# Transformer block: six modulation tiles of the mixer's stream taken during the input projection's last six output tiles, and silu(c)'s copy stored there

## The chip, the cores and the metric

The kernel runs on one core of a Trainium2 chip, in one launch. The metric is the device time of that core in microseconds (us). The engines are TensorE (PE in the profile, its weight loads PEld), VectorE (DVE), ScalarE (ACT), GpSimd (POOL) and SyncE (SP, which here issues most of the DMA transfers). Each engine works through its own list of instructions in order and waits on semaphores where it needs another's result.

## What is computed

One layer of a diffusion transformer: 512 latent tokens and 256 context tokens of width 2048, in float32.

```python
mod_l = (silu(c) @ w_ada + b_ada)          # 6 x 2048 numbers: 96 tiles of 128
mod_c = (silu(c_ctx) @ w_ada + b_ada)      # of which 32 tiles are used
sh_a, sc_a, gt_a, sh_f, sc_f, gt_f = split(mod_l, 6)
h_l = rms_norm(x) * (1 + sc_a) + sh_a      # and h_c from ctx with mod_c
qa, kva, kr, cb, cc, ch = split(h @ w_in)  # for both streams
att_l = attention(q_l, [k_l, k_c], [v_l, v_c])     # 8 heads
conv_l = cb_l * dwconv3(cc_l * ch_l)
x = x + gt_a * (rms_norm([att_l, conv_l]) @ w_out)
hf = rms_norm(x) * (1 + sc_f) + sh_f
u = dwconv3(hf @ w_up); a, g = split(u, 2)
x = x + gt_f * ((a * silu(g)) @ w_down)
return rms_norm(x)
```

The 96 tiles of mod_l are the modulation tiles: tile t is 128 columns of w_ada, multiplied by silu(c) and summed over 2048 rows. Tiles 0 to 31 (shift and scale of the mixer) are needed for h_l, 32 to 47 (gt_a) by the output projection's residual, 48 to 79 for hf, 80 to 95 at the very end.

## The kernel before, in words

The activations lie transposed in SBUF: 16 tiles of 128 features by 512 tokens. A product keeps nearly float32 accuracy by splitting each operand into a high part (a cast on ScalarE, line 166 for weights, 337 for activations) and the remainder (a subtraction on VectorE, lines 167 and 338), and takes three matmuls (lines 187 to 189: high x high, high x low, low x high). So each weight block costs one operation on ScalarE and one on VectorE before TensorE can use it.

A modulation tile isn't computed on TensorE. Its 1 MB of w_ada is loaded as two halves of 128x1024, and VectorE multiplies each half with a copy of silu(c) (`sv`, 128x2048, the same row in each partition) and sums along the row, all in one instruction with an accumulator: two dots a tile, 1.22 us each by the profile. For mod_l's tiles 0 to 31 this is line 241 in the input projection, for the context's 32 tiles line 530, for the tiles from 32 on line 263. The state of that late stream is the dictionary `late`: `late_load` starts the next tile's load, `late_dot` does one of its two dots, `late_both` both and the load of the next one. Each fourth tile the sums are added up (lines 268 and 269).

The program's phases, in order of time:

1. Start: x is loaded and squared, silu(c) becomes `sv`; then the first dots.
2. Input projection (loop at line 564). The 16 rows of the contraction are taken in three chunks `ci` of 2, 4 and 10. Per chunk, first six output tiles together (`pf`), then the other 25 of ORDER one by one (`pp`): load `rw{ci}_{m}`, split, matmuls, `evac`. In chunk 2 the context's modulation tiles (`cm`, `ctx_mods`) are dotted, one for each output tile. They run out before the last six output tiles, m = 25 to 30. Around these stand the low-rank norms (`low_rank`, line 394), the short convolution (lines 467 to 474), and the context's normalised tiles cr and hc (lines 515, 516, 343, 344).
3. Attention. It begins with the query parts pq00, pq02 and pq01 of head pair 0 (`q_nope`); pq02 is copied to `xq0` on ScalarE, and TensorE's rotation `qr0` (line 379) reads that copy. Then come the three context tiles (pc0 to pc2, weights wc), and 32 steps of softmax, in which the late stream takes 22 tiles (from t = 32 on) by 1 MB loads `ra`.
4. Output projection: 28 steps of `late_both` and `whole` take the late stream's other 34 tiles, the last of them during the halves of output tiles 14 and 15 (o140, o150, o141, o151); after that the residual (line 980), the second norm, and the preparation of hf (`hf_tile`).
5. Up projection, convolution, down projection. The last eight modulation tiles, 88 to 95, are done beside these with silu(c) loaded again from `sv_d` in DRAM (line 1291), since the SBUF space of `sv` is given up at the end of the output projection. The store to `sv_d` is line 1009.

What sets the order: a scheduler decides, by its own estimate of times, which instruction stands where on each engine's list. Only what is wrapped in `keep` holds its program order among the kept instructions of its engine: the dots of the late and the context's stream, and, until the end of chunk 1, every load of `fetch_to`. The store of line 1009 is not wrapped, and the scheduler has put it to the start of SP's list, as soon as `sv` is there. The pool `p_sb` has four buffers with the tag "ada" for the halves of modulation tiles; a load waits until the dot of the buffer's earlier content is done, and SP's list waits with it.

## Time and profile before

| what | us |
|---|---|
| median of 3 runs | 2135.92 (2135.22 to 2137.73) |
| the profiled execution, its own time | 2139.37 |
| its span, first to last instruction | 2137.6 |
| busy in it: TensorE | 2091.0 |
| VectorE | 1826.5 |
| ScalarE | 1047.5 |
| GpSimd | 117.2 |

The profile shows one execution, so its times are set against its own 2139.37 us and not against the median. A row of the timeline has the start in us, the duration, the engine, the line of the kernel, the operation, output and inputs, how many neighbouring instructions are put together, and in brackets the idle time ahead of it and what ended that. A row's duration can overlap the next row's start (the engines are pipelined), so the pitch from start to start is what a row costs in a dense stretch. A row of the windows has the stretch, its length, the busy time of PE, PEld, DVE, ACT and POOL with the number of instructions, the granted TensorE clock (1.00 is full), the DMA engines' busy share and GB/s.

### The profile page before, as it was taken

Reading aid. Unit: us, or ns where it says so; the run is one execution under the profiler, and the core shown is the slowest. Engines: PE = TensorE matmul, PEld = TensorE weight load, DVE = VectorE, ACT = ScalarE, POOL = GpSimd, SP = SyncE. Lnnn points to the kernel's source line nnn. Section 1 sums busy time; section 2 is a strip of 40 time slices with the busy share of each in tenths; the row PEclk is TensorE's granted clock in tenths of the full one; section 3 lists DMA queues with packets and bytes.
Section 4 is the critical chain, followed back from the end, with each engine's and each line's share of the span. In section 5 each row is a group of like instructions: output and inputs, shape, how many; then the busy total and the mean of one; then the engine's idle time right before and its main releaser. Section 6 shows DMA issues by size and latency. Waiting matters only on the chain.

```text
span 2137.6 us, 35318 instructions
## 1 busy us (share of the span) xinstructions
PE 2091.0 (98%) x13268; PEld 1881.8 (88%) x13268; DVE 1826.5 (85%) x3024; ACT 1047.5 (49%) x1715; POOL 117.2 (5%) x144
## 2 busy tenths in 40 slices
PE   7999999999999999999999999999999999999997
PEld 4688788888988888999999999999999889999997
DVE  7998987778896989898999999999999658888887
ACT  5533333555552337565555555555655433333445
POOL 0000000000000100011000000000000000000000
PEclk9999999999999999999999999999999999999999
DMA  8989886334459986577788888788888989878684
GB/s 331 343 279 329 276 275 195 126 128 152 166 188 353 348 283 220 142 217 207 230 238 232 233 233 244 224 234 234 235 229 229 362 306 307 250 231 239 197 236 134
DMA packets 170177, 513.75 MB, mean 240 GB/s; under 512 B 18963, under 2 KB 23315, under 8 KB 164371
## 3 DMA queue, kind: packets, MB, share of 16 engines
q1 hardware_dynamic: 133364, 418.14, 57.7%
q0 software_dynamic: 17408, 59.25, 14.1%
q10 hardware_dynamic: 19232, 34.09, 4.2%
q8 instruction: 104, 1.70, 0.3%
q14 instruction: 69, 0.56, 0.1%
HBM read 464.22 MB, written 46.14 MB: 239 GB/s over the span
## 4 chain that ended last, share of the span: by engine, by line
PE 90%; DVE 4%; DMA 3%; ACT 2%; issue 1%; SPq 0%; DVEq 0%; ACTq 0%; POOLq 0%
PE pp L187 4%; PE pp L189 4%; PE pp L188 4%; PE d L187 1%; PE o L187 1%; PE d L188 1%; PE o L188 1%; PE d L189 1%; PE o L189 1%; PE uf L187 1%; PE uf L189 1%; PE uf L188 1%; PE of L187 1%; PE of L188 1%; PE of L189 1%; PE pf L188 1%
## 5 line engine op out<-in xcount | busy, mean ns | idle before, releaser
L1151 POOL DMA_DIRECT2D u_s<-in_w_up x80 | 68.6, 857 | 684.0 <-DMA u_s<-in_w_up 378.1
L263 DVE SCALAR_TENSOR_TENSOR ada<-ada,sv 128x1024 f32<-128x1024 f32 x68 | 82.1, 1220 | 11.4 <-DMA ada<-in_w_ada 11.2
L166 ACT CAST w_0h<-rw 128x512 fp32r<-128x512 f32 (+1 forms) x63 | 38.3, 618 | 108.3 <-PE pp L188 67.6
L241 DVE SCALAR_TENSOR_TENSOR ada<-ada,sv 128x1024 f32<-128x1024 f32 x64 | 77.6, 1220 | 2.2 <-DMA ada<-in_w_ada 2.1
L530 DVE SCALAR_TENSOR_TENSOR ada<-ada,svc 128x1024 f32<-128x1024 f32 x64 | 76.0, 1219 | 2.5 <-DMA ada<-in_w_ada 2.4
L167 DVE TENSOR_TENSOR w_0l<-rw,w_0h 128x512 fp32r<-128x512 f32 (+1 forms) x63 | 42.7, 683 | 22.8 <-ACT w_0h L166 22.6
L263 DVE SCALAR_TENSOR_TENSOR ra<-ra,sv 128x1024 f32<-128x1024 f32 x44 | 52.5, 1219 | 1.1 <-DMA ra<-in_w_ada 1.1
L1265 DVE TENSOR_TENSOR u<-u,u_s 128x1024 f32<-128x1024 f32 x40 | 48.8, 1220 | 0.7 <-DMA u_s<-in_w_up 0.5
L1266 DVE TENSOR_TENSOR u<-u,u 128x1024 f32<-128x1024 f32 x40 | 48.7, 1218 | 0.0
L793 POOL TENSOR_TENSOR gr<-gr,half 128x8 f32<-128x8 f32 x4 | 10.1, 2524 | 630.1 <-DVE gr L792 538.2
L764 ACT CAST pth<-t 128x384 fp32r<-128x384 f32 x64 | 28.6, 485 | 26.4 <-PE t L761 26.4
L1075 DVE TENSOR_TENSOR tp<-a,tp 128x256 fp32r<-128x256 f32 x90 | 37.7, 419 | 3.3 <-ACT tp L1074 3.3
L1074 ACT CAST tp<-a 128x256 fp32r<-128x256 f32 x90 | 35.7, 403 | 5.5 <-DMA yl6h<-y_d 4.2
L1038 ACT ACTIVATE g<-g 128x512 f32<-128x512 f32 x43 | 27.3, 634 | 18.3 <-DVE g L1032 18.0
L541 DVE TENSOR_TENSOR acc<-acc,pp 128x512 f32<-128x512 f32 x50 | 34.1, 683 | 2.1 <-PE pp L189 2.1
L765 DVE TENSOR_TENSOR ptl<-t,pth 128x384 fp32r<-128x384 f32 x64 | 33.2, 550 | 2.6 <-ACT pth L764 2.6
L745 DVE TENSOR_REDUCE mn<-s 128x1 f32<-128x768 f32 x32 | 30.4, 953 | 4.9 <-PE s L734 4.6
L1030 ACT ACTIVATE g<-cg,sm 128x512 f32<-128x512 f32 x40 | 32.6, 815 | 0.0
L1030 ACT ACTIVATE a<-ca,sm 128x512 f32<-128x512 f32 x40 | 32.1, 802 | 0.0
L748 ACT ACTIVATE p<-s,mn 128x768 f32<-128x768 f32 x32 | 29.3, 916 | 1.6 <-DVE mn L745 1.3
L1031 DVE SCALAR_TENSOR_TENSOR g<-cg,sm,g 128x511 f32<-128x511 f32 x40 | 29.8, 746 | 0.0
L1032 DVE SCALAR_TENSOR_TENSOR g<-cg,sm,g 128x511 f32<-128x511 f32 x40 | 29.8, 746 | 0.0
(10238 smaller groups left out, 8925.0 us busy)
## 6 DMA issues: line engine op xcount, KB each, us to landing
ada<-in_w_ada SPq DMA_DIRECT2D x196, 512.0 KB, 5.7
u<-in_w_up SPq DMA_DIRECT2D x120, 512.0 KB, 8.9
w<-t_d SPq DMA_DIRECT2D x161, 256.0 KB, 5.3
u_s<-in_w_up SPq DMA_DIRECT2D x80, 512.0 KB, 4.0
u_s<-in_w_up POOLq DMA_DIRECT2D x80, 512.0 KB, 9.6
t_d<-tp ACTq DMA_DIRECT2D x126, 256.0 KB, 5.9
v<-in_w_dnw SPq DMA_DIRECT2D x72, 384.0 KB, 5.1
ra<-in_w_ada SPq DMA_DIRECT2D x22, 1024.0 KB, 4.8
```

The costliest lines, as they stand in the source:

```text
L166: A.copy(out=hi[:, :n], in_=raw[:, a:a + n])
L167: V.tensor_tensor(out=lo[:, :n], in0=raw[:, a:a + n], in1=hi[:, :n].bitcast(F32), op=ALU.subtract)
L187: PE.matmul(ps, w[0], x[0], start=first, stop=False, skip_group_check=on_top)
L188: PE.matmul(ps, w[0], x[1], start=False, stop=False, skip_group_check=on_top)
L189: PE.matmul(ps, w[1], x[0], start=False, stop=last, skip_group_check=on_top)
L241: V.scalar_tensor_tensor(out=r, in0=r, scalar=1.0, in1=vec[:, i * 1024:(i + 1) * 1024], op0=ALU.mult, op1=ALU.mult, accum_out=col[:, i:i + 1])
L263: keep(V.scalar_tensor_tensor(out=r, in0=r, scalar=1.0, in1=svs[i], op0=ALU.mult, op1=ALU.mult, accum_out=lc[:, t % 4:t % 4 + 1] if i else ...
L530: keep(V.scalar_tensor_tensor(out=raw[q], in0=raw[q], scalar=1.0, in1=svc[:, q * 1024:(q + 1) * 1024], op0=ALU.mult, op1=ALU.mult, accum_o ...
L1030: A.activation(u, src, AF.Identity, bias=s("fb", m), scale=s("fw", 86 + m))
L1151: G_.dma_start(r[-1], src[more], accum_op=ALU.add)
L1265: V.tensor_tensor(out=a11, in0=a11, in1=s1, op=ALU.add)
L1266: V.tensor_tensor(out=a12, in0=a12, in1=a11, op=ALU.add)
```

## The change

```diff
                 if ci == 2:
                     for q in range(2 if i % 4 == 0 else 1):
                         next(cm, None)
+                    if i == 18:
+                        late_load(ada_load)
+                        keep(SP.dma_start(sv_d, sv))
+                    elif i > 18:
+                        late_both(ada_load if i < len(ORDER) - G - 1 else None)
                     if i >= 5 and i % 2 == 1 and (i - 5) // 2 < CTX_EARLY:
                         bg.append(ctx_prep((i - 5) // 2))
                     pump(2)
...
     assert late["t"] == late["end"] and late["raw"] is None
-    SP.dma_start(sv_d, sv)
     ph1.close()
```

The loop variable i counts the 25 single output tiles of chunk 2; i = 18 is m = 6, and 19 to 24 are m = 25 to 30. At i = 18 the load of modulation tile 32 and the store to `sv_d`, now kept in order, are issued. At each of the six that follow, one tile is dotted (t = 32 to 37) and, except at the last, the next one loaded into the "ada" buffers. The attention then takes 38 to 59 (as many as before), and the output projection 60 to 87, 28 tiles where it took 34.

SP's list at the start of the program, before (rf00 are the first weights of the input projection, ada170 is the first half of modulation tile 17):

```order
L145 DMA ada00_235<-in_w_ada 128x1024
L145 DMA ada01_237<-in_w_ada 128x1024
L145 DMA rf00_251<-in_w_in 128x1536
L1009 DMA sv_d_81<-sv_93 128x2048
L145 DMA ada170_283<-in_w_ada 128x1024
L145 DMA ada171_285<-in_w_ada 128x1024
L145 DMA ada10_291<-in_w_ada 128x1024
```

And now, at the same place:

```order
L145 DMA ada00_235<-in_w_ada 128x1024
L145 DMA ada01_237<-in_w_ada 128x1024
L145 DMA rf00_251<-in_w_in 128x1536
L145 DMA ada170_283<-in_w_ada 128x1024
L145 DMA ada171_285<-in_w_ada 128x1024
L145 DMA ada10_291<-in_w_ada 128x1024
```

The store is gone from there. It now stands in SP's list near the end of the input projection, between the load of modulation tile 32 (ada320 and ada321) and the weights of output tile 26:

```order
L145 DMA ada150_2884<-in_w_ada 128x1024
L145 DMA ada151_2886<-in_w_ada 128x1024
L145 DMA ada320_2994<-in_w_ada 128x1024
L145 DMA ada321_2996<-in_w_ada 128x1024
L608 DMA sv_d_81<-sv_93 128x2048
L145 DMA rw2_26_3080<-in_w_in 128x1280
L145 DMA ada330_3057<-in_w_ada 128x1024
L145 DMA ada331_3059<-in_w_ada 128x1024
```

The store has moved by some 170 places in SP's list, and the loads of the late stream stand ahead of and between the weights of the last tiles.

ScalarE's list in the start, before, from the first activated tile to the first narrow weights (w0_13h and w0_15h are casts of rw0_13):

```order
L438 ACTIVATE xr0_113<-xr0_113,mod_90,sc0_244 128x512
L337 CAST h0h_247<-xr0_113 128x512
L438 ACTIVATE xr1_117<-xr1_117,mod_90,sc1_300 128x512
L166 CAST w0_13_0h_339<-rw0_13_337 128x512
L166 CAST w0_15_0h_384<-rw0_13_337 128x512
L166 CAST w0_17_0h_406<-rw0_13_337 128x512
```

And now:

```order
L438 ACTIVATE xr0_113<-xr0_113,mod_90,sc0_244 128x512
L337 CAST h0h_247<-xr0_113 128x512
L166 CAST w0_13_0h_339<-rw0_13_337 128x512
L166 CAST w0_15_0h_384<-rw0_13_337 128x512
L438 ACTIVATE xr1_117<-xr1_117,mod_90,sc1_300 128x512
L337 CAST h1h_303<-xr1_117 128x512
```

Two casts of weights have moved ahead of xr1's activation; on VectorE, in the same stretch, h0l has moved behind the three dots ada171, ada10 and ada11.

VectorE's list at the end of the input projection, before: from the context tile cr10 to qr0y, which reads the rotation qr0:

```order
L515 TENSOR_TENSOR cr10_3397<-cg5_3391,rc_220 128x256
L515 TENSOR_TENSOR cr11_3403<-cg5_3391,rc_220 128x256
L344 TENSOR_TENSOR hc10_3400<-cr10_3397,hc10_3400 128x256
L344 TENSOR_TENSOR hc11_3406<-cr11_3403,hc11_3406 128x256
L338 TENSOR_TENSOR q00l_3437<-pq00_3423,q00h_3436 128x512
L167 TENSOR_TENSOR wc00_0l_3534<-rc0_3530,wc00_0h_3533 128x512
L541 TENSOR_TENSOR acc30_710<-acc30_710,pp2_29_3259 128x512
L167 TENSOR_TENSOR wc04_0l_3551<-rc0_3530,wc04_0h_3550 128x512
L474 TENSOR_TENSOR acc30_710<-acc30_710,acc29_695 128x512
L167 TENSOR_TENSOR wc08_0l_3570<-rc0_3530,wc08_0h_3569 128x512
L381 TENSOR_TENSOR qr0y_3461<-qr0_3459,kc_83 128x512
```

And now, the same part of the list, which is longer (acc30 is the evacuation of output tile 30, ada370 and ada371 are the two halves of modulation tile 37):

```order
L515 TENSOR_TENSOR cr7_3406<-cg3_3394,rc_220 128x256
L167 TENSOR_TENSOR wq01l_3513<-rq01_3456,wq01h_3512 128x512
L541 TENSOR_TENSOR acc30_710<-acc30_710,pp2_29_3290 128x512
L263 SCALAR_TENSOR_TENSOR ada370_3324,mod_90<-ada370_3324,sv_93 128x1024
L263 SCALAR_TENSOR_TENSOR ada371_3326,lc_94<-ada371_3326,sv_93 128x1024
L471 SCALAR_TENSOR_TENSOR acc29_695<-acc28_686,sm_82,acc29_695 128x511
L344 TENSOR_TENSOR hc6_3403<-cr6_3400,hc6_3403 128x256
L344 TENSOR_TENSOR hc7_3409<-cr7_3406,hc7_3409 128x256
L167 TENSOR_TENSOR wc00_0l_3573<-rc0_3569,wc00_0h_3572 128x512
L167 TENSOR_TENSOR wc04_0l_3590<-rc0_3569,wc04_0h_3589 128x512
L472 SCALAR_TENSOR_TENSOR acc29_695<-acc28_686,sm_82,acc29_695 128x511
L167 TENSOR_TENSOR wc08_0l_3609<-rc0_3569,wc08_0h_3608 128x512
```

```order
L515 TENSOR_TENSOR cr8_3418<-cg4_3412,rc_220 128x256
L515 TENSOR_TENSOR cr9_3424<-cg4_3412,rc_220 128x256
L474 TENSOR_TENSOR acc30_710<-acc30_710,acc29_695 128x512
L344 TENSOR_TENSOR hc8_3421<-cr8_3418,hc8_3421 128x256
L344 TENSOR_TENSOR hc9_3427<-cr9_3424,hc9_3427 128x256
L515 TENSOR_TENSOR cr10_3436<-cg5_3430,rc_220 128x256
L515 TENSOR_TENSOR cr11_3442<-cg5_3430,rc_220 128x256
L344 TENSOR_TENSOR hc10_3439<-cr10_3436,hc10_3439 128x256
L344 TENSOR_TENSOR hc11_3445<-cr11_3442,hc11_3445 128x256
L338 TENSOR_TENSOR q00l_3476<-pq00_3462,q00h_3475 128x512
L381 TENSOR_TENSOR qr0y_3500<-qr0_3498,kc_83 128x512
```

Dots stand between the evacuations and what follows them, and the context tiles cr8 to cr11, which stood ahead of acc30, now stand behind it and behind the last two dots.

ScalarE's list there, before, from cr10's activation to the copy xq0:

```order
L516 ACTIVATE cr10_3397<-cr10_3397,modc_91,scc5_3395 128x256
L516 ACTIVATE cr11_3403<-cr11_3403,modc_91,scc5_3395 128x256
L343 CAST hc10_3400<-cr10_3397 128x256
L343 CAST hc11_3406<-cr11_3403 128x256
L337 CAST q00h_3436<-pq00_3423 128x512
L166 CAST wc00_0h_3533<-rc0_3530 128x512
L166 CAST wc04_0h_3550<-rc0_3530 128x512
L166 CAST wc08_0h_3569<-rc0_3530 128x512
L652 COPY xq0_3457<-pq02_3444 128x512
```

And now:

```order
L516 ACTIVATE cr10_3436<-cr10_3436,modc_91,scc5_3434 128x256
L516 ACTIVATE cr11_3442<-cr11_3442,modc_91,scc5_3434 128x256
L343 CAST hc10_3439<-cr10_3436 128x256
L343 CAST hc11_3445<-cr11_3442 128x256
L337 CAST q00h_3475<-pq00_3462 128x512
L657 COPY xq0_3496<-pq02_3483 128x512
```

The three weight casts of the first context tile (wc) stand ahead of cr8 now, and the copy follows q00h directly.

VectorE's list at the end of the output projection, before, from the last weight remainder of o151 to the residual of tile 15:

```order
L167 TENSOR_TENSOR o151w1536l_7579<-o15r1_7261,o151w1536h_7578 128x512
L263 SCALAR_TENSOR_TENSOR ada860_7370,mod_90<-ada860_7370,sv_93 128x1024
L980 SCALAR_TENSOR_TENSOR x14_7265<-ol0_7263,mod_90,x14_7265 128x256
L263 SCALAR_TENSOR_TENSOR ada861_7372,lc_94<-ada861_7372,sv_93 128x1024
L263 SCALAR_TENSOR_TENSOR ada870_7408,mod_90<-ada870_7408,sv_93 128x1024
L355 TENSOR_TENSOR fq0t_6497<-fq0t_6497,fq14_7508 128x256
L291 RECIPROCAL rr_7488<-rr_7488 128x2
L263 SCALAR_TENSOR_TENSOR ada871_7410,lc_94<-ada871_7410,sv_93 128x1024
L268 TENSOR_TENSOR mod_90<-mod_90,lc_94 128x4
L269 TENSOR_TENSOR mod_90<-mod_90,sm_82 128x4
L980 SCALAR_TENSOR_TENSOR x15_7267<-ol1_7264,mod_90,x15_7267 128x256
```

And now, from the same remainder on; the residual of tile 15 comes a few rows later:

```order
L167 TENSOR_TENSOR o151w1536l_7580<-o15r1_7292,o151w1536h_7579 128x512
L291 RECIPROCAL rr_7489<-rr_7489 128x2
L985 SCALAR_TENSOR_TENSOR x14_7296<-ol0_7294,mod_90,x14_7296 128x256
L355 TENSOR_TENSOR fq0t_6538<-fq0t_6538,fq14_7509 128x256
L962 TENSOR_TENSOR x0_6535<-x0_6535,rl_92 128x256
L962 TENSOR_TENSOR x1_6541<-x1_6541,rl_92 128x256
L282 SCALAR_TENSOR_TENSOR fs2_7860<-mod_90,sm_82 128x1
L282 SCALAR_TENSOR_TENSOR fs3_7884<-mod_90,sm_82 128x1
L967 TENSOR_TENSOR hf0l_7549<-x0_6535,hf0h_7548 128x256
L962 TENSOR_TENSOR x2_6548<-x2_6548,rl_92 128x256
L946 TENSOR_TENSOR hf10_7576<-x1_6541,hf10_7576 128x256
L962 TENSOR_TENSOR x3_6555<-x3_6555,rl_92 128x256
```

The dots are gone from there, and the first tiles of hf (x0 to x3, hf0l, hf10) have moved ahead of the residual of tile 15. TensorE's list is unchanged in its matmuls; a few of them are interleaved otherwise at the start, at the end of the input projection and at the end of the output projection.

## The prediction

> **What bounds the kernel now.** I read the busy times on the page first, then the chain of waits, then the timelines of the three places where the order of instructions differs.
>
> ```profile
> PE 2091.0 (98%) x13268; PEld 1881.8 (88%) x13268; DVE 1826.5 (85%) x3024; ACT 1047.5 (49%) x1715; POOL 117.2 (5%) x144
> PE 90%; DVE 4%; DMA 3%; ACT 2%; issue 1%; SPq 0%; DVEq 0%; ACTq 0%; POOLq 0%
> ```
>
> TensorE is busy for 98% of the span and is 90% of the chain that ends last. Its matmuls are the same before and after, so the change can only lengthen or shorten the few stretches in which TensorE waits or runs at a lower clock. VectorE, at 85%, is close behind: where it gets more work it can become what TensorE waits for. The change moves twelve dot products and twelve 512 KB loads from the output projection's end to the input projection's end, and a 1 MB store out of the start. So there are three places to price.
>
> **Place 1, the start: the store leaves a crowded SP queue.** The store's code stands at the end of the output projection, but the trace has it at the start of the program.
>
> ```profile
> 15.56 0.33 SPq L145 DMA_DIRECT2D rf<-in_w_in  x1
> 16.22 0.33 SPq L1009 DMA_DIRECT2D sv_d<-sv  x1
> 24.00:32.00 8.00, 4.11 (x13) 3.15 (x14) 7.05 (x14) 4.49 (x8) 0.00 (x0) 1.00 1.02 414
> 29.61 0.69 DVE L338 TENSOR_TENSOR h0l<-xr,h0h 128x512 fp32r<-128x512 f32 x1 [0.39 <-ACT h0h L337]
> 36.31 1.29 DVE L167 TENSOR_TENSOR w_0l<-rw,w_0h 128x512 fp32r<-128x512 f32 x2 [1.39 <-ACT w_0h L166]
> 42.29 1.22 DVE L241 SCALAR_TENSOR_TENSOR ada<-ada,sv 128x1024 f32<-128x1024 f32 x1
> 43.96 0.38 SPq L145 DMA_DIRECT2D rw<-in_w_in  x1
> DMA to landing us min/median/max: 8.5/8.9/9.2
> 52.88 0.62 ACT L166 CAST w_0h<-rw 128x512 fp32r<-128x512 f32 x1 [5.96 <-DMA rw<-in_w_in]
> 54.03 0.50 PE L187 MATMUL pp<-h0h,w_0h 128*128 128x512 f32 x1 [1.91 <-ACT acc L539]
> 57.30 0.80 PE L187 MATMUL pp<-h0h,w_0h 128*128 128x512 f32 x1 [1.23 <-ACT acc L539]
> 54.00:56.00 2.00, 1.97 (x6) 1.14 (x6) 2.00 (x5) 2.00 (x5) 0.00 (x0) 0.78 1.02 416
> 56.00:58.00 2.00, 0.77 (x3) 0.61 (x3) 2.00 (x4) 2.00 (x5) 0.00 (x0) 0.50 1.05 436
> 60.00:62.00 2.00, 2.00 (x6) 1.58 (x5) 2.00 (x8) 0.00 (x0) 0.00 (x0) 0.51 0.83 330
> ```
>
> In the window from 24 to 32 the DMA engines are full (share 1.02, 414 GB/s), so 1 MB less is about 2.5 us of transfer (1.05 MB by 414 GB/s) that everything behind it doesn't wait for. That alone gains nothing unless TensorE is held by it. It is, later: the second weight load of the narrow tiles, rw0_21, is issued at 43.96, right behind the dot that begins at 42.29 and frees a buffer in the same SP queue. It takes about 8.9 us to land, and ScalarE sits idle for 5.96 us until its cast at 52.88. Behind that cast stands the copy that frees a PSUM bank, and TensorE idles 1.91 and 1.23 us at 54.03 and 57.30 for such copies, after which the clock is 0.50.
>
> In the new order on VectorE h0l, which waited 0.39 us for its cast, stands behind three dots, and ScalarE casts the first narrow weights ahead of xr1's activation, so the 1.39 us idle at 36.31 is filled too. The dots then end 0.39 + 1.39 = 1.8 us earlier: rw0_21 is issued at about 42.2 and lands at about 51.1. ScalarE now has three casts and one activation of 0.5 to 0.7 us each ahead of the first copy (2.3 us), so that copy is at 53.4 as before, and TensorE goes on at 54.0. But the second copy, which came after three more casts and an activation, now has nothing ahead of it: TensorE goes on at about 55.6, right behind its 1.5 us of matmuls, where it was 57.30. That is **1.7 us gained**. The lower clock from 54 to 62 cost up to 3.4 us (2 x (0.22 + 0.50 + 0.50 + 0.49), the stretch from 58 to 60 taken like that before it); with one gap of 1.9 us in place of two it may vanish or stay, and I take 1.4 of it. **Term 1: -3.1.** Its bounds: 0, if the load's landing isn't brought forward; -1.7 - 3.4 = -5.1, if all of the lower clock goes.
>
> **Place 2, the end of the input projection: the dots move in.** Each dot is two rows of VectorE work; the rows before give all the pitches.
>
> ```profile
> 352.26 1.22 DVE L530 SCALAR_TENSOR_TENSOR ada<-ada,svc 128x1024 f32<-128x1024 f32 x1
> 353.41 1.22 DVE L530 SCALAR_TENSOR_TENSOR ada<-ada,svc 128x1024 f32<-128x1024 f32 x1
> 354.55 0.42 DVE L167 TENSOR_TENSOR w_8l<-rw,w_8h 128x256 fp32r<-128x256 f32 x1
> 354.89 0.68 DVE L355 TENSOR_TENSOR klt<-klt,kl 128x512 f32<-128x512 f32 x1
> 355.49 0.69 DVE L167 TENSOR_TENSOR w_0l<-rw,w_0h 128x512 fp32r<-128x512 f32 x1
> 386.40 0.40 PE L189 MATMUL pp<-h15h,w_8l 128*128 128x512 f32 x1
> sum 56.00, PE 55.20 PEld 44.59 DVE 41.67 ACT 26.56 POOL 0.00; mean PE 3.94 PEld 3.19 DVE 2.98 ACT 1.90 POOL 0.00
> 396.00:400.00 4.00, 4.00 (x19) 3.25 (x18) 3.27 (x7) 2.88 (x6) 0.00 (x0) 1.00 0.83 295
> 400.95 0.76 DVE L515 TENSOR_TENSOR cr<-cg,rc 128x256 f32<-128x256 f32 x2 [0.58 <-DMA cg<-in_ctxt]
> 403.02 0.58 ACT L337 CAST q00h<-pq 128x512 fp32r<-128x512 f32 x1
> 407.53 0.58 ACT L652 COPY xq<-pq 128x512 f32<-128x512 f32 x1
> 406.81 0.39 PE L189 MATMUL pq<-qa3h,wq02l 128*128 128x512 f32 x1
> 408.17 1.12 PE L379 MATMUL qr<-xq,kc 128*128 128x512 f32 x2 [0.97 <-ACT xq L652]
> ```
>
> A dot has a pitch of 1.15 us (352.26 to 353.41), a 128x256 operation 0.34 (354.55 to 354.89), a 128x512 one 0.60. The sum row is that of the windows from 352 to 408: VectorE is busy for 41.67 of 56 us, so it has 14.3 us free, and twelve dots take 12 x 1.15 = 13.8. On the mean they just fit; but half of them stand late. From the evacuation of tile 28 (acc28) to cr11, the new order has 45 rows on VectorE: 6 dots, 21 of 128x512, 2 of 128x511, 13 of 128x256, 3 tiny ones. That is 6 x 1.15 + 21 x 0.60 + 2 x 0.66 + 13 x 0.34 + 0.3 = 25.5 us without a single wait. Tile 28's last matmul ends at 386.8, so cr11 ends at 412.3 at the earliest; before, it was done at 401.7 (400.95 + 0.76).
>
> What hangs on cr11: ScalarE takes cr11's activation, two casts, the cast q00h, and only then the copy xq0 (in the order before three weight casts stood between q00h and the copy, now none). Before, q00h ended 1.8 us after cr11. So the copy starts at about 412.3 + 1.8 = 414.1 rather than 407.53, and TensorE's rotation (L379), which started 0.64 after the copy, at 414.7 rather than 408.17: 6.5 later. TensorE is done with its work ahead of the rotation at 407.2 (406.81 + 0.39) in both orders, and behind it stand pq01 and the context tiles. So TensorE idles some 7.5 us where it idled 0.97. The loads are not what is late: the fullest of these windows, 396 to 400, has a DMA share of 0.83. In SP's queue the store now stands ahead of tile 26's weights, and can hold them by 2.5 us at most (the transfer at the start's rate); the twelve loads wait for buffers that the dots free, and the weights of tiles 27 to 30 stand behind them. TensorE has no wait for weights here before, and a late tile would only take a part of the stall forward, since VectorE's 25.5 us stay.
>
> A wait of that length costs clock too.
>
> ```profile
> 620.97 0.36 PE L187 MATMUL po<-pth,v30h 128*128 128x256 f32 x1 [1.48 <-DVE den L791]
> 622.68 0.58 PE L188 MATMUL po<-ptl,v30h 128*128 128x256 f32 x1 [1.35 <-DVE ptl L765]
> 622.00:624.00 2.00, 1.32 (x6) 1.32 (x7) 2.00 (x5) 1.70 (x4) 0.00 (x0) 0.50 0.79 310
> 630.00:632.00 2.00, 2.00 (x6) 1.54 (x5) 2.00 (x4) 1.60 (x4) 0.00 (x0) 0.50 1.01 358
> 814.35 0.61 PE L316 MATMUL rs<-io,fq0t 128*128 128x1 f32 x4 [2.85 <-DVE fq0t L355]
> 815.83 0.39 PE L187 MATMUL uf<-hf0h,ufw0h 128*128 128x256 f32 x1 [0.88 <-ACT ufw0h L1023]
> 816.00:818.00 2.00, 2.00 (x12) 2.00 (x13) 2.00 (x5) 2.00 (x4) 0.00 (x0) 0.58 1.02 408
> 818.00:820.00 2.00, 2.00 (x12) 2.00 (x12) 2.00 (x7) 1.82 (x5) 0.00 (x0) 0.57 1.02 409
> ```
>
> After idles of 1.48 and 1.35 us the clock was 0.50 for five windows, 622 to 632: 10 us at half speed, 5.0 lost. After one of 2.85 and one of 0.88 it was 0.58 and 0.57 for 4 us: 4 x 0.425 = 1.7 lost. The new idle is a single long one, so I take the row nearest in form, 1.7, and keep 5.0 as the far end.
>
> The Trainium skill, page "TensorE: Matmul & The Clock Gate", section "Part 1: The HAM clock gate", says that the clock is halved after an idle window of about 3.4 us and restored after one of steady work, the windows running freely; by that rule the stall would cost 3.4 us at half speed, an estimate of 1.7 lost. The trace agrees at 816 to 820 and differs at 622 to 632, where the half clock followed waits of under 1.5 us and lasted three times as long.
>
> **Term 2: 6.5 + 1.7 = +8.2.** Bounds: 0, if VectorE's rows ahead of cr11 don't bind; 6.5 + 5.0 = +11.5.
>
> **Place 3, the step to the up projection: the dots leave.**
>
> ```profile
> 811.12 0.38 PE L299 MATMUL rs<-io,rr 128*128 128x128 f32 x2
> 811.27 1.23 DVE L263 SCALAR_TENSOR_TENSOR ada<-ada,sv 128x1024 f32<-128x1024 f32 x1 [0.80 <-DMA ada<-in_w_ada]
> 812.82 0.48 DVE L980 SCALAR_TENSOR_TENSOR x<-ol,mod,x 128x256 f32<-128x256 f32 x1
> ```
>
> The last matmul of the output projection is over at about 811.3, but the residual that reads it starts at 812.82, since a dot that waited for its load stands ahead of it on VectorE. TensorE's next matmul (814.35) follows the residual by 1.53. Without the dots the residual starts at about 811.4, and L316 at about 813.0 rather than 814.35; the first matmul of the up projection then waits for its weight cast and not for anything of the dots, and I put it at 814.0 rather than 815.83. **Term 3: -1.8.** Bounds: -0.5, if the weights' landing holds it; -3.5, if the 1.7 of lower clock behind it goes too (1.8 + 1.7).
>
> **Of no cost:** the store and the twelve loads in their new place (the windows' free DMA share hides them, as said), the 22 loads during the attention (as many as before), the later dots.
>
> **Sum:** -3.1 + 8.2 - 1.8 = +3.3. The profiled execution took 2139.37 us, 1.8 more than its span of 2137.6 and 3.45 more than the median of the runs, 2135.92. So it would be 2142.7 on its own scale, and 2135.92 + 3.3 = **2139.2** on that of the runs. About 0.2% (4.3 us, 2131.6 to 2140.2) is what a measurement of this kernel can tell from no change.
>
> **Rivals.**
> - *The stall doesn't arise* (chance 0.21). If VectorE has caught up before cr11, because its rows ahead of acc28 run early and the long operations overlap more than their pitch says, the second term is 0: -3.1 - 1.8 = -4.9, so 2131.0, faster. For it: the 14.3 us free against 13.8 needed. Against it: tile 28's end, from which the 25.5 us are counted, is fixed by TensorE.
> - *The half clock stays long* (0.13; the other side, slower). The mechanism of 622 to 632 at the rotation: +6.5 + 5.0 - 3.1 - 1.8 = +6.6, so 2142.5. It decides from 2.7 us of loss on (6.5 + 2.7 - 3.1 - 1.8 = 4.3), which is 5.4 us at half clock. For it: the longest stretch in the trace followed much shorter idles. Against it: the 4 us at 816.
> - *The store was not in the way* (0.14). The change doesn't gain at the start what moving the store promises: if rw0_21 waits for something else than the dots in the queue, term 1 is 0, and +8.2 - 1.8 = +6.4 gives 2142.3. For it: TensorE's first matmul waits for ScalarE's h0h rather than for a load, and the new order puts three dots ahead of h0l. Against: the 5.96 us wait at 52.88 is on a DMA.
>
> **How the numbers follow.** The forecast has 0.52, of which 0.33 lies within 0.2% and 0.19 above it, since 2139.2 is only 1.0 under the upper edge. The first rival gives 0.17 faster and 0.04 within; the second 0.13 slower; the third 0.06 within and 0.08 slower. Together faster 0.17, same 0.43, slower 0.40. The range runs from the first rival's time, less 0.5 for a start that gains more, 2130.5, to 2145.6, which is the bounds of terms 2 and 3 (+11.5 - 1.8 = +9.7) with no gain at the start; half of the first rival and the extremes of the others lie outside, under 2 in 10. The forecast's own range is 2136 to 2142.
>
> **What would show it.** At the start: rw0_21 issued at 42.2 and not 43.96, and TensorE's wait at 57.3 gone; wrong if both stay. At the input projection's end: dots on VectorE without a gap from tile 28 to cr11, the copy xq0 near 414 and a wait of 7 us at L379 (less whatever the start has gained in time), with a half clock behind it; wrong if that wait is under 3 us. At the step: the residual of x15 within 0.3 us of the last matmul. What would make the sum wrong as a whole: a wait in the attention that moves with the dots' new tile numbers, which I price at nothing.

## The result, and the profile after

| | before | changed |
|---|---|---|
| median, us (6 runs each, same chip) | 2136.38 (2134.61 to 2137.73) | 2146.47 (2141.82 to 2148.41) |
| changed / before | | 1.0045, 95% interval 1.0032 to 1.0058 |
| the profiled execution, us | 2139.37 | 2148.41 |
| its span, us | 2137.6 | 2146.5 |

The change makes the kernel slower by some 10 us; 2139.2 was forecast, with a range to 2145.6. In the profiled executions the spans differ by 8.9 us. To see where, the start of the same TensorE instruction is taken in both timelines. A difference that grows between two rows is time lost there.

| TensorE starts | before, us | changed, us | later by |
|---|---|---|---|
| chunk 1 of the input projection (pf1) | 86.18 | 83.48 | -2.70 |
| first gp5, end of output tile 29 | 393.61 | 394.58 | +0.97 |
| the rotation qr0 (L379) | 408.17 | 419.95 | +11.78 |
| first key product pkl00 | 430.92 | 445.30 | +14.38 |
| output projection (of) | 628.03 | 643.91 | +15.88 |
| up projection (uf) | 815.83 | 829.82 | +13.99 |
| down projection, sliding part (v0a) | 1756.21 | 1768.97 | +12.76 |
| last norm | 2127.03 | 2135.97 | +8.94 |

The busy times of the page look like those of before, and its chain of waits has the same shares; they don't show where 9 us went:

```profile
PE 2089.4 (97%) x13268; PEld 1878.7 (88%) x13268; DVE 1825.8 (85%) x3024; ACT 1048.9 (49%) x1715; POOL 117.1 (5%) x144
```

**The start.** The rows of the SP queue, of ScalarE, of TensorE and of the windows that answer to those of place 1, and the wait at the step into chunk 2:

```profile
42.64 0.38 SPq L145 DMA_DIRECT2D rw<-in_w_in  x1
52.27 1.14 ACT L166 CAST w_0h<-rw 128x512 fp32r<-128x512 f32 x2 [6.94 <-DMA rw<-in_w_in]
54.53 0.57 ACT L539 COPY acc<-pp 128x512 f32<-128x512 f32 x1
55.16 0.50 PE L187 MATMUL pp<-h0h,w_0h 128*128 128x512 f32 x1 [3.31 <-ACT acc L539]
56.00:58.00 2.00, 2.00 (x10) 1.44 (x9) 2.00 (x4) 1.61 (x4) 0.00 (x0) 1.00 0.81 311
223.53 0.51 PE L189 MATMUL pp<-h6h,w_0l 128*128 128x512 f32 x1 [2.01 <-DVE w_0l L167]
224.00:226.00 2.00, 2.00 (x7) 1.55 (x6) 2.00 (x4) 0.00 (x0) 0.00 (x0) 0.59 0.91 349
```

The weights rw0_21 are issued 1.3 us earlier than before, there is one wait (3.31 us) in place of two, and the clock stays at 1.00: TensorE is 2.7 us ahead at 83.48. At 223.53 it waits 2.01 us for a weight remainder of VectorE and then runs at half clock: 1.0 + 1.7 us are gone again. The same wait in the kernel before:

```profile
224.71 0.50 PE L189 MATMUL pp<-h6h,w_0l 128*128 128x512 f32 x1 [1.06 <-DVE w_0l L167]
```

**The end of the input projection.** The SP queue, ScalarE, VectorE, TensorE, windows:

```profile
390.51 1.47 SPq L145 DMA_DIRECT2D ada<-in_w_ada  x2
393.20 3.99 SPq L145 DMA_DIRECT2D rq<-in_w_q  x2
397.88 0.62 ACT L166 CAST wq02h<-rq 128x512 fp32r<-128x512 f32 x1 [2.33 <-DMA rq<-in_w_q]
398.56 0.79 PE L187 MATMUL pq<-qa0h,wq02h 128*128 128x512 f32 x1 [2.68 <-ACT wq02h L166]
406.57 0.69 DVE L167 TENSOR_TENSOR wq01l<-rq,wq01h 128x512 fp32r<-128x512 f32 x1 [2.10 <-ACT wq01h L166]
416.79 0.75 DVE L515 TENSOR_TENSOR cr<-cg,rc 128x256 f32<-128x256 f32 x2
419.32 0.58 ACT L657 COPY xq<-pq 128x512 f32<-128x512 f32 x1
419.95 2.07 PE L379 MATMUL qr<-xq,kc 128*128 128x512 f32 x2 [7.33 <-ACT xq L657]
400.00:402.00 2.00, 2.00 (x6) 1.57 (x5) 2.00 (x4) 0.00 (x0) 0.00 (x0) 0.54 0.00 0
420.00:422.00 2.00, 2.00 (x3) 0.97 (x4) 0.14 (x1) 0.00 (x0) 0.00 (x0) 0.50 0.03 8
```

Two waits stand here: 7.33 us for the copy xq0, as foreseen, and 2.68 us for the query weights wq02h, which was not. The row at 393.20 puts two loads together: the first is that of wq02, the second, at 396.86, that of wq01. The load of wq02 lands at 397.79, 4.6 us after its issue, where it took 2.6 us before. Ahead of it in the queue stands modulation tile 37 (390.51); its second half could be issued only at 391.65, when a dot had freed its buffer, and lands 0.7 us ahead of wq02. Each wait has half clock behind it. Together 2.68 + (7.33 - 0.97) + 1.6 + 2.9 (the time that TensorE worked at half clock between 398 and 402 and between 420 and 426, halved) = 13.5, and the table has 14.38 - 0.97 = 13.4.

The weights wq02 are also needed sooner than before. VectorE's remainder qa0l of the queries' first input tile and the first matmuls of wq00 and wq02, before and then now:

```profile
385.71 0.69 DVE L338 TENSOR_TENSOR qa0l<-acc,qa0h 128x512 fp32r<-128x512 f32 x1
394.42 0.48 PE L187 MATMUL pq<-qa0h,wq00h 128*128 128x512 f32 x1
397.28 0.40 PE L187 MATMUL pq<-qa0h,wq02h 128*128 128x512 f32 x1
```

```profile
399.78 0.68 DVE L338 TENSOR_TENSOR qa0l<-acc,qa0h 128x512 fp32r<-128x512 f32 x1
395.40 0.48 PE L187 MATMUL pq<-qa0h,wq00h 128*128 128x512 f32 x1
```

Before, twelve matmuls of wq00 (2.9 us) stand ahead of the first of wq02. Now there is only one, and qa0l to qa3l, which four of the others read, stand behind dots on VectorE. So the few matmuls that are interleaved otherwise bear on the cost, though no run has the dots with the order of before (and TensorE's list also differs at places in the attention, between 490 and 610 us).

**The end of the attention and the step to the up projection.** TensorE's timeline, VectorE's residual of tile 15, and a window:

```profile
630.41 0.83 PE L766 MATMUL t<-io,p 128*128 128x128 f32 x3 [2.08 <-DVE ptl L770]
639.44 0.36 PE L187 MATMUL po<-pth,v30h 128*128 128x256 f32 x1 [3.55 <-DVE ptl L770]
827.26 0.48 DVE L985 SCALAR_TENSOR_TENSOR x<-ol,mod,x 128x256 f32<-128x256 f32 x1 [0.39 <-PE ol L189]
828.87 0.61 PE L316 MATMUL rs<-io,fq0t 128*128 128x1 f32 x4 [1.65 <-DVE fq0t L355]
829.82 0.39 PE L187 MATMUL uf<-hf0h,ufw0h 128*128 128x256 f32 x1 [0.34 <-ACT ufw0h L1027]
830.00:832.00 2.00, 2.00 (x18) 2.00 (x19) 2.00 (x4) 2.00 (x4) 0.00 (x0) 1.00 0.96 351
```

At the step the residual waits for TensorE alone, the waits are 1.65 and 0.34 in place of 2.85 and 0.88, and the clock stays full: 1.7 + 1.7 us gained. At the attention's end the waits are longer than the 1.48 and 1.35 of before.

### The profile page after: what moved, and what is told of

Same layout as the page of the kernel before. It is cut to its first block, busy times and chain, and to the rows that moved or that the text cites. A ratio compares the mean times of both kernels' runs of the same rounds, so it can differ in the third digit from the quotient of the medians.

```text
span 2146.5 us, 35305 instructions
## 1 busy us (share of the span) xinstructions
PE 2089.4 (97%) x13268; PEld 1878.7 (88%) x13268; DVE 1825.8 (85%) x3024; ACT 1048.9 (49%) x1715; POOL 117.1 (5%) x144
## 4 chain that ended last, share of the span: by engine, by line
PE 90%; DVE 4%; DMA 3%; ACT 2%; issue 1%; SPq 0%; DVEq 0%; ACTq 0%; POOLq 0%
PE pp L187 4%; PE pp L189 4%; PE pp L188 4%; PE o L189 1%; PE o L188 1%; PE o L187 1%; DMA rw<-in_w_in 1%; PE d L187 1%; PE d L189 1%; PE d L188 1%; PE of L187 1%; PE uf L187 1%; PE of L188 1%; PE of L189 1%; PE uf L189 1%; PE uf L188 1%
## 5 line engine op out<-in xcount | busy, mean ns | idle before, releaser
L766 PE MATMUL t<-io,p 128*128 128x128 f32 x192 | 28.5, 275 | 2.1 <-DVE ptl L770 2.1
L1036 DVE SCALAR_TENSOR_TENSOR g<-cg,sm,g 128x511 f32<-128x511 f32 x40 | 29.8, 746 | 0.0
```

## The experiments

In the verdicts, a loss "from tile 29 to pkl" is worked out like the table above: how much later than before pkl00 starts, less how much later gp5 starts. Ratios are to the kernel before in the same comparison, with 95% intervals.

### e1 and g4: the store alone

```diff
+                    if i == 18:
+                        keep(SP.dma_start(sv_d, sv))
...
-    SP.dma_start(sv_d, sv)
```

> The kernel before with the store of silu(c) alone moved to the input projection (kept in order there); no modulation tile is moved. Theory A (the start's gain is taken away again further on, where VectorE is what TensorE waits for): TensorE is 2.5 to 2.9 us ahead at 84 us as in the changed kernel, has one wait of 3.3 us near 55 in place of two, then waits about 2.0 us for the weight remainder (L167) near 223.5 where it was 1.06, with or without a half clock of 3.4 us behind it, and is level with before by 320 us. Total 2134.5 to 2137. Rival: the start's gain lasts: 2133 to 2134 and no longer wait at 224.

> e1 once more beside these: the store moved, no tile early. The gain of the start lasts: 2 to 4 us below before; compared with g1, it lacks the gain at the step (1 to 3.5 us) and has no loss in the input projection.

e1: 2132.12 us, 0.9984 (0.9969 to 0.9999). g4, the same program in another comparison: 2133.96 us, 0.9992 (0.9982 to 1.0002). TensorE's waits in e1, then in g4, with a window each:

```profile
53.50 0.50 PE L187 MATMUL pp<-h0h,w_0h 128*128 128x512 f32 x1 [2.89 <-ACT acc L539]
54.00:56.00 2.00, 2.00 (x7) 1.52 (x7) 2.00 (x5) 1.94 (x4) 0.00 (x0) 0.58 1.02 428
222.03 0.50 PE L189 MATMUL pp<-h6h,w_0l 128*128 128x512 f32 x1 [1.30 <-DVE w_0l L167]
```

```profile
53.59 0.50 PE L187 MATMUL pp<-h0h,w_0h 128*128 128x512 f32 x1 [1.00 <-ACT acc L539]
221.37 0.59 PE L189 MATMUL pp<-h6h,w_0l 128*128 128x512 f32 x1 [2.00 <-DVE w_0l L167]
222.00:224.00 2.00, 2.00 (x6) 1.52 (x6) 2.00 (x3) 0.00 (x0) 0.00 (x0) 0.50 0.86 339
```

In e1 theory A falls: the start's gain (2.9 us at chunk 1) is still 2.7 at tile 29. In g4 the start gains 4.3 and the wait at 221 with its half clock takes 2.5 of that. One program does both: how much of the gain is left at 230 us is a matter of the execution, and g4 has the loss at 224 without any tile moved, so in the changed kernel's profile it need not come from the tiles. What stays is 1 to 3 us on the time of the run, with intervals that reach from 6.6 us below the kernel before to 0.4 above.

### e2: the six tiles alone

```diff
-                        keep(SP.dma_start(sv_d, sv))
...
+    SP.dma_start(sv_d, sv)
```

> The changed kernel with the store put back behind the output projection in the code (so that the scheduler puts it at the start again); the six tiles stay early. Theory A (the twelve dots and their loads cost the time, at two waits of TensorE: for wq02h near 398 and for the copy xq0 near 413 to 420): both waits are there (2 to 3.5 us and 6.5 to 8 us), each with half clock behind it, TensorE is 12 to 14 us later than before at the context tiles, total 2144 to 2150. Rival (the store ahead of tile 26's weights in SP's queue is what delays the end of the input projection): without it there the waits shrink by half or more, total 2136 to 2141.

2143.65 us, 1.0042 (1.0026 to 1.0058). TensorE's two waits:

```profile
397.33 0.80 PE L187 MATMUL pq<-qa0h,wq02h 128*128 128x512 f32 x1 [2.54 <-ACT wq02h L166]
417.21 2.08 PE L379 MATMUL qr<-xq,kc 128*128 128x512 f32 x2 [4.74 <-ACT xq L656]
```

The wait for wq02h is as long as with the store, that for xq0 2.6 us shorter; behind the first, half clock lasts twice as long, and TensorE comes to the rotation later. The loss from tile 29 to pkl is 11.9 us, of the 13.4 of the changed kernel. So the tiles cause the loss there, not the store; the wait for xq0 was expected at 6.5 to 8 us and is shorter. At the start the gain is gone with the store back (chunk 1 at 86.35, before 86.18).

### f1 and f2: the dots without loads, the loads without dots

f1: the early dots read a buffer that is no longer needed. f2: each early dot is taken over 8 columns.

```diff
-                        late_load(ada_load)
+                        late_load(lambda t: svcs)
...
-                        late_both(ada_load if i < len(ORDER) - G - 1 else None)
+                        late_both((lambda t: svcs) if i < len(ORDER) - G - 1 else None)
```

```diff
-                        late_both(ada_load if i < len(ORDER) - G - 1 else None)
+                        late_both(ada_load if i < len(ORDER) - G - 1 else None, 8)
```

> The changed kernel with the twelve early dots but without their loads: the dots read a buffer that lies in SBUF and is no longer needed (so six modulation tiles are not what the reference has). Theory V (VectorE's dots cost the stall at the rotation, the loads in SP's queue ahead of the query weights cost the wait for wq02h): the wait for wq02h near 396 is gone (under 0.5 us), the wait for the copy xq0 stays at 5.5 to 8 us with a half clock behind it; from the end of tile 29 to the context part pkl TensorE loses 7 to 9.5 us against before, where the changed kernel lost 13.4. Rival (the loads and the 1 MB store crowd the DMA queues and make everything late): with no loads both waits shrink under 2 us and the loss is under 3 us.

> The changed kernel with the twelve early loads, but each early dot over 8 columns in place of 1024 (so six modulation tiles are not what the reference has). Theory V: without the 13.8 us of dots VectorE is no longer behind, the wait at the rotation falls to 0.5 to 2 us; the wait for wq02h falls too (the loads no longer wait for buffers that slow dots hold), to under 1 us; loss from tile 29 to pkl 0 to 2.5 us, total 4 to 7 us below before's times, as start and step are gained. Rival (the loads): the wait for wq02h stays at 2.5 us or more, with half clock, loss of 4 us or more.

f1: 2142.33 us, 1.0037 (1.0024 to 1.0049). f2: 2132.63 us, 0.9992 (0.9977 to 1.0006). TensorE's waits in f1, then in f2:

```profile
392.59 0.50 PE L187 MATMUL pq<-qa0h,wq02h 128*128 128x512 f32 x1 [0.29 <-ACT wq02h L166]
413.44 2.08 PE L379 MATMUL qr<-xq,kc 128*128 128x512 f32 x2 [7.48 <-ACT xq L658]
```

```profile
401.73 0.39 PE L187 MATMUL pq<-qa0h,wq02h 128*128 128x512 f32 x1
405.63 1.12 PE L379 MATMUL qr<-xq,kc 128*128 128x512 f32 x2 [0.97 <-ACT xq L657]
```

f1 has TensorE's order of the changed kernel from the query weights on. With the dots and no loads the wait for wq02h is gone (0.29) and the wait for xq0 is whole (7.48); the loss is 10.6 us of 13.4, a little above what theory V gave. So the dots make most of the loss, and their loads the rest. With all the loads and the store but short dots, both waits are gone and the loss is 0.0: without slow dots the loads cost nothing here. But f2 does not show why. The scheduler, which reckons with short dots too, puts all of wq00 ahead of wq02 again, so that wq02 is first needed at 401.73, 9.5 us after its load has landed (392.22). Between f2 and the changed kernel, which differ in the length of twelve dots and in the order that goes with it, lie 0.9992 and 1.0045, some 11 us. The time of f2 is 2.1 us below that of before, where 4 to 7 had been expected.

### e3: the copy ahead of the last context tiles

```diff
-CTX_EARLY = 6
+CTX_EARLY = 4
```

> The changed kernel with only four of the context's normalised pairs prepared inside the input projection (CTX_EARLY 4 in place of 6), so that cr8 to cr11 stand behind the copy xq0 on ScalarE. Theory A (the copy stands behind cr11, and that behind VectorE's dots): the wait of 7.3 us at the rotation (L379) falls under 2 us, the wait for wq02h near 398 (2.7 us) stays, and some of the wait comes again at the context tiles pc0, which need cr8 to cr11; total 2138 to 2143. Rival (VectorE's work as a whole is late, wherever the copy stands): the same 7 to 9 us of waits at pc0 in place of the rotation, total 2145 to 2149.

2146.32 us, 1.0052 (1.0032 to 1.0073). TensorE's waits:

```profile
392.84 0.79 PE L187 MATMUL pq<-qa0h,wq02h 128*128 128x512 f32 x1 [2.83 <-ACT wq02h L166]
408.78 1.13 PE L379 MATMUL qr<-xq,kc 128*128 128x512 f32 x2 [0.97 <-ACT xq L657]
422.83 0.79 PE L187 MATMUL pc<-hc,wc_0h 128*128 128x256 f32 x2 [4.27 <-ACT hc L343]
```

Theory A, which was the prediction's own, falls here. The wait at the rotation is gone, and nothing is gained: TensorE waits 4.27 us at the context tiles (less than the 7 to 9 of the rival), with 3.4 us of clock lost around each of the two long waits, and the loss from tile 29 to pkl is 14.3 us, where the changed kernel has 13.4. The copy is only one place where VectorE's lateness came out. What CTX_EARLY = 4 costs by itself was not measured.

### f3 and f4: three and four tiles

```diff
-                    elif i > 18:
-                        late_both(ada_load if i < len(ORDER) - G - 1 else None)
+                    elif 18 < i <= 21:
+                        late_both(ada_load if i < 21 else None)
```

> The changed kernel with three early tiles (at output tiles 25, 26 and 27) in place of six; the store as in the changed kernel. Theory V: VectorE has some 7 us of waits of its own ahead of 375, which three tiles (6.9 us) fill, and no load stands between the query weights, so the wait for wq02h is gone and that at the rotation is 0.5 to 2.5 us; loss from tile 29 to pkl 0 to 2.5 us; at the step to the up projection L316 waits 1.6 to 2.4 us in place of 2.85. Total 3 to 6 us below before, below both kernels. Rival (any early tile costs its share, 13.4 / 6 = 2.2 us for each): loss of 6 to 7 us there and a total equal to before or above it.

> As f3 with four early tiles (output tiles 25 to 28). Theory V: one more tile than VectorE has room for costs 2.3 us: the wait at the rotation 2 to 4 us, none for wq02h, half clock or not; loss from tile 29 to pkl 2 to 5 us; total 2 us below before to 2 above it. Rival (share for each tile): loss 8 to 10 us.

f3: 2139.14 us, 1.0016 (1.0002 to 1.0030). f4: 2139.84 us, 1.0015 (1.0003 to 1.0028). VectorE ahead of cr10 and TensorE's waits in f3, then TensorE's waits in f4:

```profile
223.76 0.50 PE L189 MATMUL pp<-h6h,w_0l 128*128 128x512 f32 x1 [2.27 <-DVE w_0l L167]
406.89 0.69 DVE L167 TENSOR_TENSOR wc_0l<-rc,wc_0h 128x512 fp32r<-128x512 f32 x1 [1.14 <-ACT wc_0h L166]
410.66 2.08 PE L379 MATMUL qr<-xq,kc 128*128 128x512 f32 x2 [4.22 <-ACT xq L657]
```

```profile
394.36 0.49 PE L187 MATMUL pq<-qa0h,wq02h 128*128 128x512 f32 x1 [0.84 <-ACT wq02h L166]
411.99 2.07 PE L379 MATMUL qr<-xq,kc 128*128 128x512 f32 x2 [4.22 <-ACT xq L657]
```

Losses from tile 29 to pkl: 5.7 and 7.8 us. Both expectations of mine were too low, and the rival's, a share for each tile, is nearer: 1.9 us a tile for three, 1.95 for four, 1.8 for the six of f1. These are single profiles, and the share is no constant of a tile: the wait at the rotation is 4.22 us in both, and what f4 loses more is half clock (3.4 us of clock in place of 1.7) and short waits. Little of VectorE's free time in this stretch could be used in this order. In f3 VectorE itself waits 1.14 us for a weight cast ahead of cr10, so a part might have been the order; hence the next runs.

### g1, g2, g3: the dots one output tile earlier

Two tiles (g1) and three (g2), dotted from m = 6 on; g3 as g2 with CTX_EARLY = 5.

```diff
-                    if i == 18:
+                    if i == 17:
                         late_load(ada_load)
-                        keep(SP.dma_start(sv_d, sv))
-                    elif i > 18:
-                        late_both(ada_load if i < len(ORDER) - G - 1 else None)
+                    elif 17 < i <= 19:
+                        late_both(ada_load if i < 19 else None)
+                    if i == 18:
+                        keep(SP.dma_start(sv_d, sv))
```

> The changed kernel with two early tiles in place of six, dotted one output tile earlier (at m = 6 and 25, right behind the last context tile, where VectorE waits for weight casts); the store as in the changed kernel. Theory V with order (VectorE has room for these two, and xq0 stands behind wc08 as in the order before): no wait for wq02h, at the rotation 0.9 to 2 us; loss from tile 29 to pkl 0 to 1.5 us; at the step the wait for L316 is 1.6 to 2.4 us; total 2 to 6 us below before. Rival (each early tile costs about 2 us, as three cost 5.7): loss 3.5 to 4.5 us, total 1 below to 2 above before.

> As g1 with three early tiles (m = 6, 25, 26). In f3 (three tiles one output tile later) VectorE had four waits of together 4.0 us of its own between 387 and 410, so its time was not what was short; cr10 and cr11 stood behind the weight remainder of wc08, which waits for TensorE's pq. Theory O (the order): here cr10 stands ahead of wc08 and cr11 behind it, so the wait at the rotation lies between before's 0.97 and f3's 4.2: 1.5 to 3.5 us, loss 1 to 4 us. Rival (2 us a tile): loss 5.5 to 6.5 us.

> As g2 with one pair of context tiles fewer ahead of the attention (CTX_EARLY 5), so that cr10 and cr11 stand behind the copy xq0. Theory O: wait at the rotation 0.9 to 1.5 us; then a wait at pc0 for hc10 of 0 to 3 us. Loss 0 to 3 us. Rival (VectorE's work as a whole): the same 4 to 6 us of loss as f3, at pc0 in place of the rotation.

g1: 2136.63 us, 1.0011 (1.0000 to 1.0022). g2: 2138.0, 1.0011 (0.9996 to 1.0026). g3: 2138.48, 1.0011 (0.9999 to 1.0023). ScalarE and TensorE in g1:

```profile
364.49 0.62 ACT L166 CAST w_0h<-rw 128x512 fp32r<-128x512 f32 x1 [7.12 <-DMA rw<-in_w_in]
365.16 0.50 PE L187 MATMUL pp<-h6h,w_0h 128*128 128x512 f32 x1 [2.24 <-ACT w_0h L166]
411.06 1.13 PE L379 MATMUL qr<-xq,kc 128*128 128x512 f32 x2 [0.97 <-ACT xq L658]
```

At the rotation g1 has the wait of before, and no loss from tile 29 on. But its weights come late behind the modulation tiles' loads and the store in SP's queue: a wait of 2.24 us and half clock, 4.0 us lost ahead of tile 29. g2 and g3 have the same wait (1.98 and 1.72) and lose 3.7 and 3.5 us there; from tile 29 to pkl they lose 3.2 and 1.2, with 2.75 and 0.97 us of wait at the rotation. So theory O's figures for this stretch held in all three, but they decide little: while TensorE was held up ahead of it, VectorE had nearly 4 us more time. The total of g1, expected 2 to 6 us below before, is 1.4 above.

### h1 and h2: three and two tiles with cr10 and cr11 behind the copy

f3 with CTX_EARLY = 5 (h1), and the same with two tiles (h2).

> f3 (three early tiles at m = 25 to 27) with one pair of context tiles fewer ahead of the attention (CTX_EARLY 5), so that cr10 and cr11, which in f3 stood behind wc08 and ahead of the copy xq0, stand behind the copy; nothing else is changed, and no load stands ahead of the weights of tile 25. Theory O (of f3's 5.7 us the most is the order, not VectorE's time): wait at the rotation 0.9 to 1.6 us, no wait of over 1 us ahead of it or at pc0; loss from tile 29 to pkl 0 to 2 us; total 2 to 6 us below before. Rival (VectorE's time): the loss stays at 4 to 6 us, wherever the wait stands; total equal to f3.

> As h1 with two early tiles (m = 25 and 26). Theory O: as h1, loss 0 to 1.5 us, wait for L316 1.6 to 2.4 us; total 2 to 6 us below before. Rival (VectorE's time, 2 us a tile): loss 3 to 4.5 us.

h1: 2137.22 us, 1.0010 (0.9997 to 1.0024). h2: 2138.89, 1.0023 (1.0013 to 1.0033). TensorE's waits in h1:

```profile
403.51 1.13 PE L379 MATMUL qr<-xq,kc 128*128 128x512 f32 x2 [0.96 <-ACT xq L658]
418.55 0.39 PE L189 MATMUL pc<-hc,wc_0l 128*128 128x256 f32 x1 [0.64 <-DVE wc_0l L167]
```

No long wait is left. From tile 29 to pkl 2.3 us are lost (h1) and 1.9 (h2), where f3 lost 5.7: there theory O comes nearer than its rival, though its 0 to 2 us are missed. Up to the first attention product (po) it is 4.2 and 3.6, where f3 lost 5.6. What is left are short waits: two at the context tiles (0.35 and some 0.65) and one of 1.17 us for the context's keys, 0.46 before. They are the same with two tiles as with three, so they look like the price of CTX_EARLY = 5; but no run has that alone, and how much of f3's loss was the order and how much VectorE's time stays open. One tile more costs 0.5 to 0.6 us here, not 2. In the totals nothing is gained: 2.8 and 4.4 us above before, where 2 to 6 below had been expected.

### e4: the dots earlier within the output projection

e1 with a second modulation tile from output tile 7 on:

```diff
-often=m > 9
+often=m > 6
```

> The kernel before with the store moved as in e1, no tile in the input projection, and the output projection taking a second modulation tile more often (from output tile 7 on, not 10), so that the dots end ahead of the last halves. Theory A (what the change gains at the step to the up projection, 1.8 us of wait and 1.7 us of half clock, needs only that the dots are gone from there): wait for L316 about 1.6 us in place of 2.85, no half clock at 816 to 820, no new wait inside the output projection, total 2131 to 2134.5. Rival (VectorE, 85 to 94% busy in the output projection, can't take the dots sooner): new waits of TensorE there, total 2136 or more.

2139.93 us, 1.0020 (1.0009 to 1.0031). SP's queue and TensorE:

```profile
789.84 1.96 SPq L145 DMA_DIRECT2D o15r<-in_w_out  x2
797.04 0.58 PE L187 MATMUL ol<-mx0h,o150w0h 128*128 128x256 f32 x1 [8.37 <-ACT o150w0h L166]
818.97 0.61 PE L316 MATMUL rs<-io,fq0t 128*128 128x1 f32 x4 [1.72 <-DVE fq0t L355]
```

The gain at the step is there (1.72 at L316), so it needs only that the dots are gone. But the weights of the last output tile, issued at 784.1 before, now stand behind six more loads and come at 789.84: a wait of 8.37 us. The rival had the right sign. VectorE acts by way of the queue: between 776 and 792 SP waits 10.3 us in all for dots to free the buffers of these loads.

Of all these only e1, the store alone, is below the kernel before by more than its comparison is uncertain, and in its repetition g4 the interval just reaches 1.

## Why the prediction was wrong

1. **Term 1, the start (-3.1).** Near in sum, and that is luck. The profile has -2.7, e1 -2.9, g4 -4.3. The load came earlier and one of the two waits is gone, as said. But the wait left was 3.31 us, as long as the two before together (1.91 + 1.23), since the load took 9.6 us and the first copy came at 54.53 and not 53.4; so the 1.7 us of waits weren't gained. In their place the whole half clock fell away, 3.4 us, of which 1.4 had been taken. The sum counts the gain to the end: that held in e1 and not in the profiled execution.
2. **Term 2, the end of the input projection (+8.2).** Here is the step that failed. The count of rows was good: from acc28 to cr11 there are 45, and they took 26.3 us in f1 and 28.9 in the changed kernel, of which 0.5 and 2.9 were waits; 25.5 without a wait had been counted. The wait at the rotation was 7.48 us in f1 and 7.33 in the changed kernel, and 7.5 had been forecast. What failed is the sentence "The loads are not what is late". The load of wq02 came late behind that of tile 37, and TensorE, which now wants wq02 after one matmul and not after twelve, waited 2.68 us for it and lost 1.6 at half clock: 4.3 us that had been priced at nothing. f1 shows it: without the loads that wait is 0.29. The reason that was given, that a late tile "would only take a part of the stall forward, since VectorE's 25.5 us stay", failed with it. VectorE waited for TensorE in its turn: 2.10 us at 406.57 for the cast of wq01, which ScalarE could do only after a matmul of tile 30. So both came later by about as much, and the second wait kept its length. The rest is half clock behind the rotation, 2.9 in place of 1.7, still inside its bounds.
3. The mechanism within term 2 was only half right. The prediction hung the loss on the copy behind cr11; e3 took the copy out and lost as much (CTX_EARLY = 4 may have a price of its own in it). It is the dots on VectorE that cost (f1 10.6 us, f2 none), and they come out at several places: the copy, the queries' inputs, the context tiles. That twelve dots fit into 14.3 us of free time "on the mean" says little: f3, f4 and f1 paid 1.8 to 1.95 us of TensorE for each tile, out of the 2.3 us of VectorE that it takes. With another order the price of one tile more was smaller (0.5 us between h1 and h2).
4. **Term 3, the step (-1.8).** Right in its place, under-sized: -3.4, near the bound of -3.5 that had been given, since the half clock went as well.
5. **"Of no cost."** The attention's end lost 1.5 us in the table (14.38 to 15.88), with waits of 2.08 and 3.55 us on VectorE. f2, with loads and short dots, has waits of the same length there and lost 1.9 (its lateness goes from -2.5 to -0.7), so it is not the dots of the input projection. Every run with early tiles has a longest wait of 1.8 to 3.6 us there, and e1, e4 and g4, which have none, 1.5 as before. So it goes with the tiles' move, as the prediction's last sentence had it ("a wait in the attention that moves with the dots' new tile numbers"). What it costs is open: e2 has the tile numbers of the changed kernel and gained 0.5 us between the same two rows, f4 gained 1.0, and the half clock there varies from 1.7 to 5.1 us.
6. **Rivals.** "The stall doesn't arise" was given 0.21 and is refuted. "The half clock stays long" came partly true: it was 1.2 us more than taken. "The store was not in the way" is refuted by e1 and g4, which gain at the start, and by e2, which does not. The case that happened, a second wait ahead of the first that adds to it, was not among them.
7. Together, in the profiled executions: -2.7 at the start, +2.7 at 224 and +1.0 more up to tile 29, +13.4, +1.5, -3.1 from there to the down projection with the step in it, and -3.8 in the down projection, which does not look like an effect of the change (below): 8.9.

## What to carry to other kernels

Free time of an engine, summed over a stretch, is not yet room for more work: ask at each inserted operation which instruction stands next in line behind it, and who waits for that. A load inserted into a queue can cost more by what stands behind it than by its bytes, above all where it must wait for a buffer (8.37 us in e4). Where two engines wait for each other, a wait of one is not taken off the other's. And a store that nothing needs soon can be placed by the scheduler where the queues are fullest; keeping it out of the start was the one part of this change that may have paid, by 1 to 3 us.

## What was not expected of the hardware

Half clock came in whole stretches. In every profile here but for its last 15 us, a stretch of it cost close to 1.71, 3.41 or 5.12 us of clock, that is one to three windows of 3.4 us at half speed (1.71 at 224 and 398 in the changed kernel; 5.12 at 415, of which 2.9 fell on work and the rest on the wait itself). The Trainium skill, page "TensorE: Matmul & The Clock Gate", section "Part 1: The HAM clock gate", gives a free-running window of 3.4 us, and that agrees. It says that the clock is halved after at least one idle window; here shorter waits were enough, and not always: 2.00 us at 221 in g4 brought a window, 1.30 in e1 and, by f3's windows, 2.27 at 223 did not. In these profiles waits of 1 to 3 us so cost themselves alone, or 1.7 us of clock more (2.68 in the changed kernel), or 3.4 (2.54 in e2, 2.83 in e3), or 5.1 (1.48 and 1.35 close together before, at 622). It is one source of scatter: up to 2100 us e1 lost 5.1 us of clock and g4, the same program, 8.5.

The sliding part of the down projection ran at different speeds at full clock. Here are the windows from 1760 to 2060 of before, and then of e1, whose order on the engines is the same there; the count behind PE's busy time is that of matmuls:

```profile
1760.00:2060.00 300.00, 299.44 (x2495) 299.22 (x2494) 254.51 (x377) 120.39 (x147) 16.22 (x19) 1.00 0.82 245
```

```profile
1760.00:2060.00 300.00, 300.00 (x2528) 299.88 (x2528) 256.49 (x376) 122.67 (x151) 17.07 (x20) 1.00 0.82 246
```

2495 matmuls against 2528 in the same 300 us, at a granted clock of 1.00. From v0a to the last norm of the table the sixteen profiles took 364.9 to 371.5 us, without regard to what had been changed: f3, f4 and e3 near 371, e1, g4 and the changed kernel near 367. TensorE's order is the same in all of them there. Its cause wasn't sought. It makes 3.8 us of the profiled executions' difference, and is one reason why single profiles are to be compared stage by stage and kernels by medians.
